# RMSNorm and matmul on one core: all loads from tile 16 on in halves of eight tiles, the last stores cut smaller

## The chip, the core and the metric

The kernel runs on one core of a Trainium2 chip. The metric is device time in microseconds (us), of which lower is better. A core has five engines with an instruction stream each: TensorE (PE) multiplies matrices, VectorE (DVE) and ScalarE (ACT) work element by element, GpSimd (POOL) casts here, and SyncE (SP) only issues transfers (DMAs) between the DRAM and the on-chip memory. All transfers of this kernel but one of 2 KB are issued from SP, in the order of its stream, and are carried out by 16 DMA engines.

## The reference

`x` has 16 x 1024 rows of 512 numbers, `weight` is 512 x 768, `gamma` has 512 numbers (ones), all in float32:

```
rms    = np.sqrt(np.mean(x ** 2, axis=-1, keepdims=True) + eps)
x_norm = x / rms * gamma
return np.matmul(x_norm, weight).astype(np.float32)
```

So 33.6 MB of `x` are read and 50.3 MB of output are written.

## The kernel before

The 16384 rows are worked on in NT = 128 tiles of 128 rows. A group of `x` has XG = 16 tiles (4 MB), a group of outputs OG = 8 tiles (3 MB). Inside a group of `x` a partition holds 16 consecutive rows, so that the part of one load or store that belongs to a partition is one stretch of DRAM: 32 KB for a load of 16 tiles, 16 KB for a load of 8, 24 KB for a store of 8 tiles, 12 KB for 4 and 6 KB for 2.

The path of a tile: the load brings `x` in float32 into one of two buffers `xt`. POOL casts it to bfloat16 (`cast`, L186, and `cast_quad`, L258). ACT squares it and sums each row (`square`, L194); for a batch of tiles ACT takes the root and DVE the reciprocal (`root`, L199 and L201). The cast rows are turned so that the features stand on the partitions: for twelve tiles of sixteen by PE (`transpose_word`, L228) with a copy by DVE (`evac`, L237), for the other four (a quad) by 16 block transposes on DVE (`move_quad`, L269). PE then multiplies with the weights (`matmuls`, L298), eight products for each tile, into one of three accumulators. Last, ACT (even tiles, L277) or DVE (odd tiles, L279) multiplies with the reciprocal root and writes to one of three buffers `ot` (`finish_tile`), and `store` (L291) issues the transfer out when the last tile of its stretch is done.

The order of all work is written out by hand in one list and given to the class `Order`. It finds from the cells that an operation reads and writes which earlier operations it has to wait for, leaves out waits that follow from waits already made, gives each transfer a semaphore slot, and emits the streams. `emit` returns the transfers that nobody waited for, and SP waits for those at the very end (L437).

Two tables say how the groups are cut. `x_size` gives the size of each load: group 0 goes in loads of 2, 2, 4 and 8 tiles, the groups 1, 2, 5, 6 and 7 in two loads of eight, and the groups 3 and 4 (tiles 48 to 63 and 64 to 79) in one load of sixteen. `o_size` gives the size of each store: group 0 in 2, 2, 4 tiles, group 1 in 4, 4, the last group (120 to 127) in 4, 4, all others in one store of eight.

Loop: `for j in range(1, NP)` works on a pair of tiles, 2j and 2j+1. `load_until` at its head issues the loads of a whole group as soon as the loop is 20 tiles or less ahead of it: the loads of group 3 stand in SP's stream behind the store of tiles 16 to 23, those of group 4 behind the store of tiles 32 to 39. A load waits until the tiles that lay in its buffer were read. The squares of pair j+4 are in ACT's stream ahead of the finish of tile 2j.

To keep a store to one wait, the finish of the last tile of a stretch also waits for the tile before it (`before` in `finish_tile`).

Of the kernel before, what the change touches and what calls it, by code (L numbers as in the profile page):

```python
# [20 lines left out]
class Order:  # L21
# [17 lines left out]
    def emit(self):  # L39
        nc = self.tc.nc  # L40
        streams = {id(e): n for n, e in enumerate((nc.tensor, nc.vector, nc.scalar, nc.gpsimd, nc.sync))}
        writer, readers = {}, {}
        known = [dict() for _ in streams]
        clocks, needs, place, slot_of, slots = [], [], [], {}, []
        count = [0] * len(streams)
        for n, (proc, engine, _, reads, writes) in enumerate(self.ops):
            at = streams[id(engine)]
            if proc is None:
                me, turn = ("transfer", n), 1
            else:  # L50
                count[at] += 1
                me, turn = at, count[at]
            written = {writer[cell] for cell in reads + writes if cell in writer}
            read = {d for cell in writes for d in readers.get(cell, ())}
            need = []
            for d in sorted(written | read, reverse=True):
                who, when = place[d]
                if who == me and (engine is nc.tensor or d not in written):
                    continue
                if known[at].get(who, 0) < when:  # L60
                    need.append(d)
                    for k, v in clocks[d].items():
                        known[at][k] = max(known[at].get(k, 0), v)
            if proc is None:
                free = [k for k, d in enumerate(slots) if known[at].get(("transfer", d), 0)]
                if free:
                    slots[free[0]] = n
                else:
                    slots.append(n)
                slot_of[n] = ("slot", slots.index(n))  # L70
            clock = dict(known[at])
            clock[me] = turn
            place.append((me, turn))
            clocks.append(clock)
            needs.append(need)
            for cell in reads:
                readers.setdefault(cell, []).append(n)
            for cell in writes:
                writer[cell], readers[cell] = n, []
        awaited = {d for need in needs for d in need}  # L80
        last = [n for n, (me, _) in enumerate(place) if not isinstance(me, int) and n not in awaited]
        sems, marks, done = {}, {}, {}
        for n in range(len(self.ops)):
            me = slot_of.get(n, place[n][0])
            if n in slot_of or n in awaited:
                if me not in sems:
                    sems[me] = self.tc.alloc_semaphore(f"done{len(sems)}")
                done[me] = done.get(me, 0) + (16 if n in slot_of else 1)
                marks[n] = (sems[me], done[me])
        for n, (proc, engine, issue, _, _) in enumerate(self.ops):  # L90
            for d in needs[n]:
                engine.wait_ge(*marks[d])  # L92
            ins = issue()
            if n in marks:
                ins.then_inc(marks[n][0], 16 if n in slot_of else 1)
        return [marks[n] for n in last]
# [3 lines left out]
def kernel(  # L100
# [18 lines left out]
    _, O = out.shape  # L119
    K = D // P  # L120
    NT = N // P
    NP = NT // 2
    XG, OG = 16, 8
    AHEAD = 20

    def stretches(group, parts):
        first, size, i = {}, {}, 0
        for g in range(NT // group):
            for n in parts.get(g, [group]):
                for t in range(i, i + n):  # L130
                    first[t], size[t] = i, n
                i += n
        return first, size

    last = NT // OG - 1
    x_first, x_size = stretches(XG, {0: [2, 2, 4, 8], **{g: [8, 8] for g in (1, 2, 5, 6, 7)}})
    o_first, o_size = stretches(OG, {0: [2, 2, 4], 1: [4, 4], last: [4, 4]})

    def rows(ap, i, n):
        base, t = (x_first[i], x_size[i]) if i < XG else (i - i % XG, XG)  # L140
# [332 lines left out]
```

## Time and profile before

| what | value |
|---|---|
| time, median of 5 runs (lowest to highest) | 209.91 us (209.66 to 210.12) |
| time of the profiled execution | 209.65 us |
| its span in the profile | 207.7 us |
| PE, DVE, ACT, POOL busy | 193.0, 149.3, 144.4, 59.9 us |
| DMA: bytes, mean rate | 85.62 MB, 412 GB/s |
| SP's queue (q1), share of 16 engines' span | 97.2% |
| transfers of x: 16 tiles / 8 tiles | 2 / 11 |
| stores: 8 / 4 / 2 tiles | 13 / 5 / 2 |
| last store issued | at 199.54 us |

The page cuts the span into 40 slices of 5.2 us. In the rows of digits 9 stands for 90% or more of a slice. "Idle before" names what an engine waited for last. The chain that ended last is followed back from the last instruction and says on which engine or transfer the time was spent. Beside that page the trace can be asked for the waits, for the busy time of each engine in any stretch, and for every instruction in order of time; it also holds a record of each DMA packet (start, duration, bytes) and of each landing: a transfer leaves 16 landings, one for each DMA engine.

### The profile page before, as it was taken

To read this page: it belongs to the slowest core of one execution; us is meant where nothing else is said; L and a number is where in the kernel's file an instruction comes from. 1 tells how busy PE (TensorE), PEld (TensorE's weight loads), DVE (VectorE), ACT (ScalarE), POOL (GpSimd) and SP (SyncE) were. 2 spreads that over 40 slices of the span, in tenths; PEclk is the share of its full clock that TensorE was granted. 3 is DMA by queue.
4 is the path that set the end of the run, shared out by engine and by line. 5 is a ranking of instruction groups with operands and counts; after the bars stand their busy time and mean duration, and the time that the engine had idled before them with its cause. 6 is when DMAs were issued, how large, how long until landed. Compare 5 with 4: busy or idle time off the path is not lost.

```text
span 207.7 us, 2760 instructions
## 1 busy us (share of the span) xinstructions
PE 193.0 (93%) x1212; PEld 72.3 (35%) x717; DVE 149.3 (72%) x255; ACT 144.4 (70%) x343; POOL 59.9 (29%) x34
## 2 busy tenths in 40 slices
PE   7789999999999999998999999999999999999920
PEld 1134444433334333342344333433343334343300
DVE  0455647998489956998569975999569984999410
ACT  4698897777768397865977688677877788663310
POOL 3247642046300192005800670006600273000000
PEclk9999999999999999999999999999999999999995
DMA  6999999999999999999999999999999999996995
GB/s 226 425 451 413 357 401 422 437 439 427 433 445 442 375 448 440 432 412 429 448 405 423 434 450 434 412 424 432 448 412 417 435 450 429 431 426 265 450 381 230
DMA packets 5488, 85.62 MB, mean 412 GB/s; under 512 B 610, under 2 KB 612, under 8 KB 1380
## 3 DMA queue, kind: packets, MB, share of 16 engines
q1 hardware_dynamic: 5472, 85.46, 97.2%
q8 instruction: 7, 0.11, 0.2%
q14 instruction: 5, 0.04, 0.0%
q10 hardware_dynamic: 4, 0.00, 0.0%
HBM read 35.13 MB, written 50.33 MB: 411 GB/s over the span
## 4 chain that ended last, share of the span: by engine, by line
PE 71%; DMA 16%; DVE 5%; issue 2%; SPq 1%; ACT 1%; POOL 1%; ACTq 0%
PE ps L298 62%; DMA xt<-in_x_dram 16%; PE ps L228 8%; DVE ot L279 2%; DVE xTq L269 2%; DVE xT L237 1%; POOL xb L186 1%; ACT jk L194 0%; SPq L343 0%; SPq L175 0%; ACT ot L277 0%; SPq L291 0%; DVE rstd L201 0%; SPq L468 0%; ACTq L92 0%
## 5 line engine op out<-in xcount | busy, mean ns | idle before, releaser
L298 PE MATMUL ps<-w_bf,xT 128*128 128x256 bf16 (+1 forms) x783 | 145.1, 325 | 2.7 <-DVE w_bf L279 0.8
L277 ACT ACTIVATE ot<-ps,rstd 128x768 f32<-128x768 f32 x64 | 57.5, 898 | 42.5 <-PE ps L298 40.8
L194 ACT ACTIVATE jk<-xt 128x512 bf16<-128x512 f32 x128 | 78.8, 619 | 7.8 <-DMA xt<-in_x_dram 7.8
L186 POOL CAST xb<-xt 128x2048 bf16<-128x2048 f32 (+3 forms) x21 | 46.3, 2221 | 112.3 <-DMA xt<-in_x_dram 94.8
L279 DVE TENSOR_SCALAR ot<-ps,rstd 128x768 f32<-128x768 f32 x64 | 64.8, 1013 | 9.6 <-PE ps L298 8.9
L294 PEld LDWEIGHTS <-xT 128*128 128x128 bf16 x400 | 39.3, 98 | 60.5 <-issue 52.4
L228 PE MATMUL ps<-ident_f,xb 128*128 128x128 f32 x200 | 54.2, 274 | 1.0 <-POOL xb L186 0.9
L237 DVE COPY xT<-ps 128x1024 bf16<-128x1024 bf16 (+1 forms) x53 | 34.5, 653 | 23.9 <-PE ps L228 22.2
L269 DVE STREAM_TRANSPOSE xTq<-xq 32x256 f32<-32x256 f32 x112 | 48.8, 435 | 3.4
L228 PEld LDWEIGHTS ps<-ident_f,xb 128*128 128x128 f32 x200 | 28.0, 141 | 46.6 <-issue 42.7
L298 PE MATMUL ps<-w_bf,xTq 128*128 128x256 bf16 (+1 forms) x217 | 41.8, 324 | 0.4
L194 ACT ACTIVATION_READ_ACCUMULATOR jk<-xt 128x1 f32 x128 | 24.3, 190 | 0.0
L294 PEld LDWEIGHTS <-xTq 128*128 128x128 bf16 x112 | 11.0, 98 | 14.5 <-issue 14.5
L258 POOL CAST xq<-xt 128x2048 bf16<-128x2048 f32 x7 | 13.3, 1897 | 0.0
L201 DVE RECIPROCAL rstd<-rms 128x8 f32<-128x8 f32 (+3 forms) x20 | 3.8, 192 | 8.4 <-ACT rms L199 8.2
L199 ACT ACTIVATE rms<-ssq,eps_sb 128x8 f32<-128x8 f32 (+3 forms) x20 | 6.0, 300 | 0.7
L298 PE MATMUL ps<-warm 128*128 128x512 bf16 x10 | 3.9, 531 | 1.4 <-DVE eps_sb L352 1.4
L277 ACT ACTIVATE w_bf<-w_f,g_sb 128x768 bf16<-128x768 f32 x2 | 1.9, 936 | 1.2 <-DMA w_f<-in_weight_dram 1.2
L375 DVE COPY g_sb<-ps 128x4 f32<-128x4 f32 x1 | 0.2, 161 | 3.1 <-PE ps L369 3.1
L339 ACT ACT_TABLE_LOAD x1 | 1.3, 1283 | 1.5 <-SPq L432 1.5
L279 DVE TENSOR_SCALAR w_bf<-w_f,g_sb 128x512 bf16<-128x512 f32 (+2 forms) x3 | 1.4, 481 | 0.7 <-DMA w_f<-in_weight_dram 0.7
L369 PEld LDWEIGHTS ps<-ident_f,g_row 2*128 2x128 f32 x2 | 0.3, 200 | 2.6 <-issue 2.6
(10 smaller groups left out, 1.9 us busy)
## 6 DMA issues: line engine op xcount, KB each, us to landing
out_dram<-ot SPq DMA_DIRECT2D x13, 3072.0 KB, 15.2
xt<-in_x_dram SPq DMA_DIRECT2D x11, 2048.0 KB, 19.7
xt<-in_x_dram SPq DMA_DIRECT2D x2, 4096.0 KB, 23.5
out_dram<-ot SPq DMA_DIRECT2D x5, 1536.0 KB, 11.2
w_f<-in_weight_dram SPq DMA_DIRECT2D x2, 768.0 KB, 5.6
out_dram<-ot SPq DMA_DIRECT2D x2, 768.0 KB, 15.9
xt<-in_x_dram SPq DMA_DIRECT2D x2, 512.0 KB, 5.2
xt<-in_x_dram SPq DMA_DIRECT2D x1, 1024.0 KB, 9.1
```

The costliest lines, as they stand in the source:

```text
L186: run(POOL, lambda: POOL.tensor_copy(out=xb[s][:, i % 8:i % 8 + n, :], in_=src), of, cells("xb", s, i % 8, n))
L194: run(ACT, lambda: ACT.activation(out=jk[j], in_=src[:, 0, :], func=AF.Square, accum_out=ssq[:, i:i + 1]), of, [("jk", j), ("ssq", i)])
L199: run(ACT, lambda: ACT.activation(out=rms[:, s], in_=ssq[:, s], func=AF.Sqrt, scale=1.0 / D, bias=eps_sb), [("ssq", t) for t in range(i, i ...
L201: run(DVE, lambda: DVE.reciprocal(out=rstd[:, s], in_=rms[:, s]), [("rms", i)], [("rstd", t) for t in range(i, i + n)])
L228: run(PE, lambda: PE.transpose(out=tp[b][:, t, h, :], in_=words[:, lo:lo + P], identity=ident_f), cells("xb", s, j % 4 * 2 + t) + ["ident" ...
L237: run(DVE, lambda: DVE.tensor_copy(out=dst[:, t:t + n, :], in_=src[:, t:t + n, :]), [("tp", b)], cells("xT", j % 4, t, n))
L258: run(POOL, lambda: POOL.tensor_copy(out=xq[s], in_=src), of, [("xq", s)])
L269: run(DVE, lambda: DVE.transpose(out=dst, in_=src), [("xq", s)], [("xTq", s)])
L277: run(ACT, lambda: ACT.mul(out=dst, in_=src, mul=r), reads, writes)
L279: run(DVE, lambda: DVE.tensor_single_scalar(out=dst, in_=src, scalar=r, op=mybir.AluOpType.mult), reads, writes)
L294: run(PE, lambda: PE.ldweights(lhsT), [cell])
L298: run(PE, lambda: PE.add_instruction(mybir.InstMatmult(name=nc.get_next_instruction_name(), engine=mybir.EngineType.PE, ins=[PE.lower_ap(r ...
```

## The change

Three places. The groups 3 and 4 of `x` are loaded in two loads of eight tiles, as the others are. The store of tiles 112 to 119 is cut into two of four tiles, and the second of the last group (124 to 127) into two of two tiles. And `emit` decides in another way which transfers are left for SP to wait for at the end: those whose completion stands in no engine's `known` clock, in place of those that no operation waits for.

```
-        last = [n for n, (me, _) in enumerate(place) if not isinstance(me, int) and n not in awaited]
+        seen = {who for clock in known for who in clock}
+        last = [n for n, (me, _) in enumerate(place) if me not in seen and not isinstance(me, int)]
...
-    x_first, x_size = stretches(XG, {0: [2, 2, 4, 8], **{g: [8, 8] for g in (1, 2, 5, 6, 7)}})
-    o_first, o_size = stretches(OG, {0: [2, 2, 4], 1: [4, 4], last: [4, 4]})
+    x_first, x_size = stretches(XG, {0: [2, 2, 4, 8], **{g: [8, 8] for g in range(1, NT // XG)}})
+    o_first, o_size = stretches(OG, {0: [2, 2, 4], 1: [4, 4], last - 1: [4, 4], last: [4, 2, 2]})
```

## The prediction

> **What bounds the kernel now.** I began with the page: busy shares, the slices, the queues.
>
> ```profile
> PE 193.0 (93%) x1212; PEld 72.3 (35%) x717; DVE 149.3 (72%) x255; ACT 144.4 (70%) x343; POOL 59.9 (29%) x34
> ...
> DMA  6999999999999999999999999999999999996995
> GB/s 226 425 451 413 357 401 422 437 439 427 433 445 442 375 448 440 432 412 429 448 405 423 434 450 434 412 424 432 448 412 417 435 450 429 431 426 265 450 381 230
> ...
> q1 hardware_dynamic: 5472, 85.46, 97.2%
> ...
> PE 71%; DMA 16%; DVE 5%; issue 2%; SPq 1%; ACT 1%; POOL 1%; ACTq 0%
> ```
>
> PE is busy for 93%, and the chain names it for 71%. But SP's queue fills the 16 DMA engines for 97.2%; from the second to the 36th slice the DMA row has only nines. Two resources are nearly full, and the question is which sets the end. PE's last product ends at about 198.5 us, DVE finishes tile 127 at 199.51, and the last landing is at 206.30. So I looked at the only hole of the DMA row, the 37th slice, us by us (columns: stretch, length, busy time and count of each engine, clock, DMA share, GB/s):
>
> ```profile
> 186.00:187.00 1.00, 0.97 (x7) 0.34 (x4) 0.97 (x2) 0.43 (x1) 0.00 (x0) 1.00 0.91 393
> 187.00:188.00 1.00, 0.98 (x7) 0.40 (x4) 0.92 (x3) 0.47 (x1) 0.00 (x0) 1.00 0.69 295
> 188.00:189.00 1.00, 1.00 (x8) 0.29 (x3) 0.95 (x2) 0.00 (x0) 0.00 (x0) 1.00 0.46 197
> 189.00:190.00 1.00, 1.00 (x8) 0.29 (x3) 0.97 (x2) 0.61 (x1) 0.00 (x0) 1.00 0.17 74
> 190.00:191.00 1.00, 1.00 (x8) 0.29 (x3) 0.93 (x3) 0.29 (x1) 0.00 (x0) 1.00 0.98 418
> ```
>
> The share falls step by step, 0.91, 0.69, 0.46, 0.17: the engines run dry one after another, not together. The landings say the same. Of the store of tiles 104 to 111 the first engine's part lands at 187.51, the median at 189.09, the last at 191.47. The packet records say why. In 13 stores of eight tiles nearly every 24 KB packet took 912 ns, but on one engine, in an unbroken chain, 92 packets had a mean of 945 ns; its 12 KB packets took 482 where the others' took 460. This late engine loses 8 x 0.033 = 0.26 us in each such store, 3.4 us over 13, so its 3.96 us of delay are explained. It closes its part of that store at 190.98 us; two others, delayed by instruction fetches and slow packets, at 190.81 and 190.72. The next store (tiles 112 to 119) was issued at 189.78 and its first packets start at 190.6. Thirteen engines had stood idle; the late one went on without a pause, and it is last in every later landing: 198.97, 202.68, 206.30, each 0.6 us behind the field. The end of the kernel is this one engine's queue, full from 2 us to the end.
>
> **The change part by part.**
>
> *Groups 3 and 4 in halves.* Here the waits around 60 to 100 us:
>
> ```profile
> POOL xb L186 <- DMA xt<-in_x_dram: 35.0, 2, 18.0
> ...
> ACT jk L194 <- DMA xt<-in_x_dram: 5.4, 2, 3.0
> ...
> PE ps L298 <- ACT ot L277: 0.7, 1, 0.7
> ```
>
> ACT's first square of group 3 waits 2.38 us for its load, that of group 4 3.00 us (ready at 92.94, load landed at 95.86); behind it stands the finish of tile 56, and PE misses its accumulator for 0.7 us. A load of 16 tiles is eight packets of 1213 ns on each engine, 9.7 us; its first half lands 4.9 us sooner, so both ACT waits go, and PE's 0.7 us. What is late next? The transfers: each store would be issued up to 0.7 us sooner, but a store waits 7 us or more behind others (median 15.2 us to landing where eight packets of 912 ns are 7.3). PE's 0.7 us is worth nothing at the end as long as the queue is full. The last store is issued at 199.54 and the late engine reaches its packets at about 205.8 - 8 x 0.48 = 202.0: some 2 us of cover. Were that gone, the 0.7 us would count in full.
>
> The price: two packets of 16 KB for one of 32, 2 x 611 - 1213 = 9 ns, eight times, and one closing packet of 9 ns for each further transfer: 0.08 us on each engine for a group, 0.16 for both. SP issues a second load in about 0.87 us (0.86 and 0.87 where a group is halved today); the store next in its stream waits for a tile some 10 us later (59.07 after 48.55), so nobody is kept. POOL and ACT wait once more for each group, on a load that in the halved groups lands before the square comes round: 0, covered until the second half comes over 4 tiles, 6 us, late.
>
> *Tiles 112 to 119 in two stores.* The store of 112 to 115 is issued when DVE is done with tile 115, at 183.45 us, 6.3 us sooner, and fills the hole: 0.09 + 0.31 + 0.54 + 0.83 = 1.8 us of mean idle. But it fills it on the engines that were early. On the late engine the same bytes follow without a pause now, so its gain is 0, and its price is the packets': 16 x 482 against 8 x 945 ns and one closing packet, 0.16 us. A gain of 190.98 - 190.62 = 0.36 us, down to the others' start, would be there only for the 0.6 us by which it ends last, and needs it to be less late: excluded from the sum, kept in a rival.
>
> *Tiles 124 to 127 in two stores.* Tiles 124 and 125 leave when DVE is done with 125, at 196.9, not 199.5; the late engine then still has the stores ahead until 202. So again no gain. 6 KB packets: 234 ns against 460 for 12 KB, 8 ns a pair elsewhere; for the late engine no row shows 6 KB packets in a full write queue, so from 2 x 241 (the slowest ordinary one at 28 us) to 2 x 256 (its 22 ns added to each): 0.0 to 0.24 us. I take 0.07, nearest to the 8 ns a pair.
>
> The two cut stores add a wait of DVE on ACT at tile 115 and at 125: ACT is done with 114 at 181.40 before DVE starts at 182.43, and with 124 at 195.49 before 195.89. Cost 0, with 0.4 us of margin in the second. On SP nothing but the next stores is queued behind the new ones.
>
> *Fewer waits at the end.* A transfer enters a `known` clock only when an operation waits for it or inherits that from one that did. So "in nobody's clock" and "waited for by nobody" are the same set, and this edit does nothing. The unawaited stores are those of the last use of each `ot` buffer: four before, six after. The extra waits are met while the last store is under way: SP waits 5.9 us for that one. Cost 0; the 207.7 - 206.3 = 1.4 us after the last landing stay.
>
> *Sum on the late engine:* 0.16 + 0.16 + 0.07 = 0.39, say +0.4 us (0.3 to 0.6). From the profiled 209.65 that is 210.05; its time is 0.26 under the median of 209.91, and it is the median that will be compared, so 210.3.
>
> The Trainium skill speaks louder against the change: "SBUF: State Buffer", section "The DMA setup-cost knee", gives every transfer a fixed cost of about 2 us and says to coalesce into the largest transfer; four more would make 8 us by it, an estimate of 217.9. The rows here stand against that: in the full queue a closing packet takes 9 ns and the next transfer's first packet starts at once.
>
> **The rivals.**
>
> *Faster: the hole counts.* If the late engine's delay were less in the runs than in the profile, or the engines shared their delay, filling the hole would bring the mean idle of 1.8 us, less 0.4: 208.5. At most the last 768 KB store would be bound by PE: issue 198.8, 0.5 to its first packet, eight of 234 ns, 0.5 to land, 202.1, or 4 us less. For it: the hole is real, and the mean of the 16 engines is 1.8 us early. Against it: the last landing follows the late engine without a pause, and the runs without a profile (209.66 and up) are not faster than the profiled one, as they would be if it were less late there.
>
> *Slower: a read stall on a late engine.* Single load packets took up to twice their time at moments when the other engines turned from a load to a store, and hit engines already late: +0.54 us at 47 us, +1.06 and +0.83 at 68, +0.61 at 142. Every transfer after 48 us is now timed anew. If one more such stall falls on any of the three late engines (two stand only 0.3 and 0.4 us behind the last), it goes straight to the end: 0.4 + 0.5 to 1.1, that is 210.8 to 211.4. It decides from a stall of 0.3 us on. It can also go the other way, as the one at 68 us fell into a 4 MB load that is now cut.
>
> *It does not do what it says.* For the waits I hold that as certain, and it is in the sum.
>
> **How the numbers follow.** What a measurement here can tell from no change is about 0.2%, 0.42 us. Forecast (late engine bound, +0.3 to +0.6 with a spread of the runs of 0.25): 0.60, its own range 209.9 to 210.9; of that 0.36 lies within 0.42 us and 0.24 above. Hole counts: 0.24, 206.1 to 209.0, mostly near 208.5. Stall: 0.14. The rest, 0.02, no change. So faster 0.24, same 0.38, slower 0.38. The range from 208.3 to 211.1 leaves out some 0.10 of the second case and 0.05 of the third.
>
> **What would show it.** Right: PE's wait of 0.7 us and ACT's of 3.0 and 2.38 us gone; the DMA share at 0.9 or more from 186 to 191 us; the engines then running dry at the very end, the share falling over the last 4 us before the last landing and that store's 16 landings spread by about 4 us instead of 0.6, with the last one still near 206.5. Wrong: a last landing below 205.7 with its 16 landings close together (the hole counted), or a late engine more than 4.5 us behind (the stall).

## The result, and the profile after

Median 210.18 us (209.93 to 211.7, 22 runs) against 209.88 us for the kernel before (209.51 to 210.5, 40 runs): a ratio of 1.002, 95% interval 1.0011 to 1.003. The kernel became slower by 0.3 us going by the medians, by 0.2 to 0.6 us going by the ratio: clear of zero, and about as much as the 0.2% that the prediction counted as no change. Two of the 22 runs took 211.47 and 211.7 us, where none of the 40 runs of the kernel before took more than 210.5. Beside later kernels it was timed once more: 1.0014 (1.0001 to 1.0027). The profiled execution took 210.05 us with a span of 208.0.

The page after: busy shares, the DMA rows of the slices, SP's queue, and the chain by engine.

```profile
PE 193.5 (93%) x1212; PEld 72.8 (35%) x717; DVE 149.3 (72%) x255; ACT 144.7 (70%) x343; POOL 60.0 (29%) x34
...
DMA  6999999999999999999999999999999999999991
GB/s 224 381 444 422 394 411 424 446 429 424 440 418 432 435 424 430 433 427 425 429 422 427 451 419 438 421 419 441 424 432 435 430 414 443 440 421 416 423 396 65
...
q1 hardware_dynamic: 6048, 85.46, 97.2%
...
PE 88%; DMA 5%; SPq 1%; issue 1%; POOL 1%; DVE 0%
```

The hole of the 37th slice is gone, and nothing was won by it. Note the chain: it gives PE 88% now, although PE does not set the end (experiment e5). The chain follows an instruction's waits; that a transfer lay in a full queue is not in it.

Us by us, the stretch where the hole was and the end (columns as before):

```profile
186.00:187.00 1.00, 0.95 (x7) 0.41 (x4) 0.93 (x3) 0.88 (x1) 0.00 (x0) 1.00 0.97 418
187.00:188.00 1.00, 1.00 (x9) 0.32 (x5) 0.94 (x3) 0.02 (x1) 0.00 (x0) 1.00 1.01 430
188.00:189.00 1.00, 1.00 (x8) 0.32 (x4) 0.97 (x2) 0.06 (x1) 0.00 (x0) 1.00 0.98 418
189.00:190.00 1.00, 1.00 (x8) 0.32 (x4) 0.93 (x3) 0.84 (x1) 0.00 (x0) 1.00 1.07 455
...
202.00:203.00 1.00, 0.00 (x0) 0.00 (x0) 0.00 (x0) 0.00 (x0) 0.00 (x0) 0.50 0.72 301
203.00:204.00 1.00, 0.00 (x0) 0.00 (x0) 0.00 (x0) 0.00 (x0) 0.00 (x0) 0.50 0.41 172
204.00:205.00 1.00, 0.00 (x0) 0.00 (x0) 0.00 (x0) 0.00 (x0) 0.00 (x0) 0.50 0.15 61
205.00:206.00 1.00, 0.00 (x0) 0.00 (x0) 0.00 (x0) 0.00 (x0) 0.00 (x0) 0.50 0.10 43
```

The staircase that stood at 186 to 190 us (0.91, 0.69, 0.46, 0.17) has moved to the very end: 0.72, 0.41, 0.15, 0.10. The engines run dry one after another there. The 16 landings of the last store run from 202.58 to 206.43, over 3.85 us; before, from 205.70 to 206.30. Fourteen engines finish sooner by 0.8 us or more, the last two, at 206.12 and 206.43, do not. The slow chain of store packets is there as before: 92 packets of 24 KB with a mean of 945 ns.

### The profile page after: what moved, and what is told of

The parts are those of the page before. It is cut to its first block, busy times and chain, and to the rows that moved or that the text cites. A ratio compares the mean times of both kernels' runs of the same rounds, so it can differ in the third digit from the quotient of the medians.

```text
span 208.0 us, 2771 instructions
## 1 busy us (share of the span) xinstructions
PE 193.5 (93%) x1212; PEld 72.8 (35%) x717; DVE 149.3 (72%) x255; ACT 144.7 (70%) x343; POOL 60.0 (29%) x34
## 4 chain that ended last, share of the span: by engine, by line
PE 88%; DMA 5%; SPq 1%; issue 1%; POOL 1%; DVE 0%
PE ps L299 78%; PE ps L229 10%; DMA xt<-in_x_dram 5%; POOL xb L187 1%; DVE ot L280 0%; SPq L344 0%; SPq L176 0%; SPq L469 0%; SPq L433 0%
## 5 line engine op out<-in xcount | busy, mean ns | idle before, releaser
L299 PE MATMUL ps<-warm 128*128 128x512 bf16 x10 | 4.8, 627 | 1.4 <-DVE eps_sb L353 1.4
```

The source lines that it names most:

```text
L299: run(PE, lambda: PE.add_instruction(mybir.InstMatmult(name=nc.get_next_instruction_name(), engine=mybir.EngineType.PE, ins=[PE.lower_ap(r ...
```

## The experiments

Each kernel is named by its difference. A ratio is to the kernel before, timed on the same chip.

**e1: the loads alone**

```
-    ... {g: [8, 8] for g in (1, 2, 5, 6, 7)}
+    ... {g: [8, 8] for g in range(1, NT // XG)}
```

> The kernel before with one part of the change: groups 3 and 4 of x in two loads of eight. Theory (the end is set by the latest of the 16 DMA engines, whose queue is full from 2 us on): PE's 0.7 us wait near 97 us is gone, and nothing of it reaches the end; two further transfers cost 2 x 0.08 us, so +0.0 to +0.3 us against before, and the hole in the DMA share near 188 us stays or grows by up to 0.7 us. Rival (PE's chain sets the end): 0.7 us less.

Measured: 1.0008 (0.9996 to 1.0019), 209.95 us. PE's wait of 0.7 us on ACT is gone from its waits, and so are ACT's two waits for the whole loads. ACT's waits for loads over the whole span were, in the kernel before,

```profile
ACT jk L194 <- DMA xt<-in_x_dram: 7.8, 5, 3.0
```

and here they are

```profile
ACT jk L194 <- DMA xt<-in_x_dram: 3.0, 3, 1.7
```

Tile 127 is done at 198.46 instead of 199.51, 1.05 us sooner; the last landing is at 206.28 instead of 206.30. The hole is still there (a DMA share of 0.63 and 0.52 from 187 to 189 us). A sooner PE is worth nothing at the end. The interval rules out the rival's 0.7 us.

**e2: the stores alone**

```
-    ... 1: [4, 4], last: [4, 4]})
+    ... 1: [4, 4], last - 1: [4, 4], last: [4, 2, 2]})
```

> The kernel before with the other part alone: tiles 112 to 119 stored in 4, 4 and 120 to 127 in 4, 2, 2. Theory of the latest engine: the hole near 188 us is filled, the landings of the last store are spread by about 4 us instead of 0.6, and the last landing stays: +0.0 to +0.4 us. Rival (the hole counts): 1.4 to 1.8 us less.

Measured: 1.0012 (0.9998 to 1.0027), 210.01 us. Its end, us by us:

```profile
202.00:203.00 1.00, 0.00 (x0) 0.00 (x0) 0.00 (x0) 0.00 (x0) 0.00 (x0) 0.50 0.98 406
203.00:204.00 1.00, 0.00 (x0) 0.00 (x0) 0.00 (x0) 0.00 (x0) 0.00 (x0) 0.50 0.46 190
204.00:205.00 1.00, 0.00 (x0) 0.00 (x0) 0.00 (x0) 0.00 (x0) 0.00 (x0) 0.50 0.19 80
205.00:206.00 1.00, 0.00 (x0) 0.00 (x0) 0.00 (x0) 0.00 (x0) 0.00 (x0) 0.50 0.12 49
```

The hole is filled (0.90 or more from 185 to 191 us), the staircase stands at the end, and the last store's landings go from 203.28 to 206.79. The 1.4 to 1.8 us of the rival are ruled out.

The third part, the rule for the last waits, had no run of its own. By the code of `emit`, the old and the new rule pick the same transfers, four in the kernel before and six in the kernel after, and nothing else depends on the rule.

**e4: less in the queue**

```
-        if i == first + n - 1:
+        if i == first + n - 1 and i != 63:
```

> The kernel after without the store of tiles 56 to 63, whose rows stay unwritten: 3 MB less in the queue near 95 us, 7.3 us of work for an ordinary engine and 7.6 us for the late one. Theory of the latest engine: the queue's end moves forward until PE binds: last store issued at about 199, then 0.5 us to its first packet, eight of 0.24 us and 0.5 us to land, so 3.5 to 4 us less than after. Rival (PE's chain sets the end): under 0.5 us less.

Measured: 205.76 us, 0.98 (0.9783 to 0.9817), so 4.4 us under the kernel after, a little more than the 3.5 to 4 that were expected. Its last us:

```profile
200.00:201.00 1.00, 0.00 (x0) 0.00 (x0) 0.00 (x0) 0.00 (x0) 0.00 (x0) 0.53 1.05 436
201.00:202.00 1.00, 0.00 (x0) 0.00 (x0) 0.00 (x0) 0.00 (x0) 0.00 (x0) 0.50 0.54 215
202.00:203.00 1.00, 0.00 (x0) 0.00 (x0) 0.00 (x0) 0.00 (x0) 0.00 (x0) 0.50 0.00 0
```

The share stays at 1.05 and drops to nothing within one us: all 16 landings of the last store lie between 201.94 and 202.16. The queue ran dry before (a share of 0.01 from 193 to 194 us), and the engines started level. Now PE sets the end: the store of tiles 120 to 123 is issued when tile 123 is done, at 193.27, and from there the last packets follow one another to the end. The work of PE is the same and 3 MB less are in the queue. That 4.4 us are to be had this way shows that the queue bounds the kernel after; PE comes next, 4.4 us below it.

**e5: more on PE**

```
+            if i == 100:
+                hold(warm[:, :P], "warm")
+                for _ in range(10):
+                    product(ops[a][:, :WIDE], warm[:, :P], warm, True, True, ["warm"], [("ops", a, 0)])
             matmuls(i, a, range(K), feed)
```

> The kernel after with one more weight load and ten more products of 512 columns on PE ahead of tile 100, written into an accumulator that is overwritten next: 2.2 us of PE work more at about 155 us. Theory of the latest engine: PE and the last store's issue are 2.2 us later, the last store still reaches the late engine before that has worked off its queue (4 us of cover), and the time is as in after, within 0.3 us. Rival (PE's chain sets the end): 2.2 us more.

Measured: 210.23 us, 1.001 (0.9998 to 1.0022); the kernel after has 210.18. PE is busy for 196.1 us instead of 193.5. The end in order of time:

```profile
199.52 1.02 DVE L280 TENSOR_SCALAR ot<-ps,rstd 128x768 f32<-128x768 f32 x1 [1.58 <-PE ps L299]
200.56 0.33 SPq L292 DMA_DIRECT2D out_dram<-ot  x1
```

Of the 2.6 us, 1.5 reach the end of PE's work: the last store is issued at 200.56 instead of 199.09, not 2.2 us later as was expected. The last landing comes 6 us after that issue, at 206.80, and the time of the runs is that of the kernel after. An engine that is 93% busy took 2.6 us more work, and finished 1.5 us later, for nothing; the interval excludes 1.5 us more. With e4 this settles what binds: each of the two resources was changed by itself, and only the queue moved the time.

**e7: the price of a transfer**

```
+            for p in range(first, first + n, 2 if n == OG else n):
+                m = 2 if n == OG else n
+                src = ot[s][:, p % OG:p % OG + m, :]
+                order.transfer(SP, ... rows(out, p, m) ..., reads=cells("ot", s, p % OG, m))
```

> The kernel after with each of the 12 stores of eight tiles (tiles 16 to 111) issued as four transfers of two tiles one behind the other, at the place in SP's stream where the one stood: 36 transfers more, and no load is pushed back. It prices a transfer in the full queue. By the packets (8 x (4 x 234 - 912) and three closing packets of 9 ns): 0.22 us for each store on an ordinary engine, 2.6 us over all; on the late engine between 0 and 6 us. So 2 to 4 us above after, PE without a new stall. By a fixed cost of about 2 us each: 72 us.

Measured: 214.4 us, 1.021 (1.017 to 1.0251). The kernel before had 210.1 on that chip, so the kernel after would have had about 210.4: 4.0 us for 36 transfers, 0.11 us each. On the first engine the last landing moved from 202.58 to 204.89, 2.3 us (2.6 were worked out); on the last one from 206.43 to 210.35, 3.9 us. PE waited more than was expected (2.4 us for ACT), but the DMA share is 0.97 or more from 184 to 193 us, so the queue covered it. So a transfer in a full queue costs its packets, not 2 us.

**e3: the same cuts in another place**

```
-    ... 1: [4, 4], last: [4, 4]})
+    ... 1: [4, 4], **{g: [2, 2, 2, 2] for g in range(2, last + 1)}})
```

> The kernel before with all stores from tile 16 on in pieces of two tiles: 41 transfers more, in size as the last two of the change. Theory (a transfer costs a full queue only its packets): on the late engine 0.18 to 0.66 us for each of 13 cut stores, on the others 0.22, so 2.5 to 8 us more, most likely 3 to 5. By a fixed cost of about 2 us for each transfer: 80 us more. If filling the queue sooner were worth something: less than before.

Measured: 1.0292 (1.0264 to 1.0319), 216.34 us. That is 6.4 us, inside the expected 2.5 to 8, but packets alone are not the reason, for PE stalls here. SP's queue, and the wait behind it:

```profile
35.67 20.71 SPq L291 DMA_DIRECT2D out_dram<-ot  x8
56.42 1.10 SPq L175 DMA_DIRECT2D xt<-in_x_dram  x1
```

```profile
PE ps L298 <- ACT ot L277: 6.7, 3, 5.6
```

SP issues in order. A store of two tiles is waited for at each pair, so group 3's load, which stood behind the store of tile 23, now stands behind that of tile 29 and is issued at 56.42 instead of 48.55. The move of the loads is in this number together with the 41 transfers; e7, where the four transfers are issued at the old place, gives the price of the transfers alone. The change itself is free of this: no load follows the stores that it cuts.

**e6: taking the late engine out**

```
+            low = 0
+            for high in CUTS.get(first, []) + [P]:
+                order.transfer(SP, ... rows(out, first, n)[low:high], in_=src[low:high] ...)
+                low = high
...
+    CUTS = {32: [120], 48: [126], 64: [104], 80: [108], 96: [110]}
```

> The kernel after with five stores of eight tiles each cut by partitions into two transfers, so that ever fewer DMA engines may take part: tiles 32 to 39 as 120 and 8 partitions, 48 to 55 as 126 and 2, 64 to 71 as 104 and 24, 80 to 87 as 108 and 20, 96 to 103 as 110 and 18. If the number of engines is the largest up to 16 that divides the partitions, and the first ones are taken, the engines left out get 8 to 10 packets of 24 KB less in each, and the first two 12 more over all, 10.9 us. Theory of the latest engine: the time is now set by the first engines, 7 us (if the late engines are among the last) to 11 us (if they are among the first) above after. Rival (the mean of the engines or PE sets the end): under 2 us more.

Measured: 256.29 us, 1.221 (1.2181 to 1.2238), 46 us more than before, far outside both expectations. Its DMA rows:

```profile
DMA  6999999999999989999999898998986669994840
GB/s 261 439 435 389 373 435 431 414 444 422 433 431 288 292 318 396 420 348 351 351 405 375 295 342 317 387 351 277 318 308 282 243 188 255 321 359 191 355 193 17
```

From the first such store on (72 us) the engines are busy but slow: 9 at 288 GB/s. In the packet records, 263 of the 1291 packets of 24 KB after 75 us took more than one and a half times 912 ns, with a mean of 2.06 us. The number of engines was as assumed: the transfer of 120 partitions leaves 15 landings beside one update at its issue, that of 8 leaves eight beside one. (The Trainium skill, "DMA: Bandwidth & Descriptors", section "Why a DMA increments its semaphore by 16 and not by 1", gives that rule: the number of engines is the largest up to 16 that divides the partitions, and the issuing engine writes the rest of the 16 at once. These counts agree with it, and so do those of the other four stores.) Why the packets collide was not tried, and which of the 16 is the late engine stays open.

**e8: the same cut where every engine runs dry**

```
 (as e4)
-    ... last - 1: [4, 4], last: [4, 2, 2]})
+    ... last: [4, 4]})
```

> The kernel after without the store of tiles 56 to 63 (rows unwritten, as before in e4_store_left_out) and with the uncut last stores of the kernel before (120 to 127 in 4 and 4, 112 to 119 in one). Where no engine is late, the cut of the last store should be worth what it promises: this kernel ends with 1.5 MB after PE is done where e4_store_left_out ends with 0.75 MB, so 1.6 to 2.0 us slower than that. If the cut is worth nothing whether or not an engine is late: equal to it.

Measured: 208.27 us, 0.9908 (0.988 to 0.9936), against 0.98 for e4: 2.3 us slower by the ratios, 2.7 by the last landings (204.89 and 202.16), more than the 1.6 to 2.0 that were expected. The expectation counted the last store alone, but the hole counts as well: here 16.1 us lie between the issue of the uncut store of tiles 112 to 119, at 188.81, and the last landing, while in e4 8.9 us lie between the issue of the store of tiles 120 to 123, at 193.27, and the last landing. The share in the hole:

```profile
185.00:186.00 1.00, 1.00 (x8) 0.37 (x5) 0.97 (x2) 0.40 (x1) 0.00 (x0) 1.00 0.12 49
186.00:187.00 1.00, 0.95 (x7) 0.40 (x4) 0.93 (x3) 0.50 (x1) 0.00 (x0) 1.00 0.00 0
187.00:188.00 1.00, 1.00 (x8) 0.29 (x3) 0.94 (x3) 0.00 (x0) 0.00 (x0) 1.00 0.00 0
188.00:189.00 1.00, 1.00 (x8) 0.29 (x3) 0.97 (x2) 0.58 (x1) 0.00 (x0) 1.00 0.00 0
```

Here no engine has work for three us. One is still late, for the landings of tiles 104 to 111 run from 184.84 to 186.61, but its part too has landed 2.2 us before the next store is issued. In the kernel before the share fell no lower than 0.17: three engines in sixteen were still busy, and that made the same cut worthless.

**e9 and e10: fewer transfers, and where the cover ends.** If transfers cost and PE is covered, fewer of them should be faster than both kernels.

```
 (e9, from the kernel before)
-    ... {g: [8, 8] for g in (1, 2, 5, 6, 7)}
-    ... {0: [2, 2, 4], 1: [4, 4], last: [4, 4]}
+    ... {g: [8, 8] for g in (1, 2, 7)}
+    ... {0: [2, 2, 4], last: [4, 4]}
 (e10: the same with)
+    ... {0: [2, 2, 4], last - 1: [4, 4], last: [4, 2, 2]}
```

> The kernel before turned the other way: groups 3, 4, 5 and 6 of x each in one load of sixteen tiles, and tiles 8 to 15 stored in one piece, so three transfers fewer than before. Theory (a full queue pays for packets, PE has some 2 us of cover): at 0.08 to 0.11 us each, 0.2 to 0.4 us less than before, although ACT waits 2 to 3 us for each whole load and PE up to 0.7 us. Rival (the waits of PE count): 0.7 to 1.5 us more.

> e9_fewer_transfers with the cut last stores of the kernel after (112 to 119 in 4, 4; 124 to 127 in 2, 2). In e9 PE is 3.3 us later, and the store of tiles 112 to 119, issued at 193.0, came after even the late engine had run dry. Theory: with that store cut, its first half is there in time, the queue stays full, and the time is that of the late engine again, as in after, 210.0 to 210.5. If instead PE's 3.3 us count whatever the cut: 212 and more.

Measured: e9 212.18 us, 1.0097 (1.0079 to 1.0115); e10 210.46 us, 1.0019 (1.0003 to 1.0034). The expectation for e9 was wrong: tile 127 is done 3.3 us later than before, and this time it counts. PE waits 3.4 us for ACT instead of 0.7, and at the start 0.6 us more for the weights. Around the hole of e9:

```profile
189.00:190.00 1.00, 1.00 (x9) 0.45 (x5) 0.97 (x2) 0.17 (x1) 0.00 (x0) 1.00 0.29 123
190.00:191.00 1.00, 1.00 (x9) 0.36 (x4) 0.93 (x3) 0.74 (x1) 0.00 (x0) 1.00 0.12 49
191.00:192.00 1.00, 1.00 (x7) 0.29 (x3) 0.94 (x2) 0.00 (x0) 0.00 (x0) 1.00 0.00 0
192.00:193.00 1.00, 1.00 (x8) 0.30 (x4) 1.00 (x1) 0.35 (x1) 0.00 (x0) 1.00 0.00 0
```

The uncut store of tiles 112 to 119 is issued only at 193.05, when even the late engine is dry; from there 14.7 us of packets follow. In the kernel before, the late engine went on to this store at 190.98, 0.4 us after the first packets of it had started, so 2.9 of the 3.3 us should reach the end. The last landing is at 209.14, 2.84 us later than before. With that store cut, in e10, the first half is there in time:

```profile
189.00:190.00 1.00, 0.99 (x7) 0.40 (x4) 0.90 (x3) 0.46 (x1) 0.00 (x0) 1.00 0.87 369
190.00:191.00 1.00, 1.00 (x8) 0.29 (x3) 0.97 (x2) 0.00 (x0) 0.00 (x0) 1.00 1.04 442
```

The queue as a whole does not stay full in e10: the share is 0.70 and 0.73 from 191 to 193 us and 0.35 from 196 to 197. The last engine's queue does: from the store of tiles 104 to 111 on, the last landings of the stores are at 191.94, 195.71, 199.46, 203.21, 205.07 and 206.89, one stretch of packets after another. The other fifteen engines land the last store between 205.01 and 205.49.

So the cut of the tail is worth nothing in the kernel before, 2.3 us in e8, and e10 is 1.6 us faster than e9. Not all of that is the cut's: in the profile of e10 tile 127 is done 2.0 us later than before, not 3.3. PE's wait for ACT is 2.7 us there instead of 3.4, which is 0.7 of the difference; the rest was not followed. None of the kernels that do the whole computation beat the kernel before.

**e11: the kernel after again**

> The kernel after once more, beside e10 on the same chip: 210.1 to 210.4, 1.0011 to 1.003 of the kernel before.

Measured: 210.25 us, 1.0014 (1.0001 to 1.0027). Its last store's landings run from 202.38 to 206.63.

## Why the prediction was right, step by step

- *What binds.* Right, and shown: the queue (e4, -4.4 us), not PE (e5, no change). The late engine is no matter of one execution: in the profiles of before, after, e1, e2, e5, e9, e10 and e11 the last engine's part of the store of tiles 104 to 111 lands 3.0 to 4.5 us behind the first one's. Why one engine is slower is open.
- *The halves of groups 3 and 4.* Right: the waits are gone, PE is sooner, the end is not (e1).
- *The cut of tiles 112 to 119 and of 124 to 127.* Right: the hole is filled on the engines that were early, and the last engine's queue is unchanged (e2; landings of the kernel after). The condition that the prediction gave, that a late engine still has work when the next store comes, is shown by its opposite in e8.
- *The rival "hole counts".* Ruled out for this kernel by e2. It holds as soon as all engines run dry (e8, e9). The 202.1 us in the prediction's bound for it is added up wrongly: its terms make 201.7, so the low end of that rival's range, 206.1, stands 0.4 us too high. No result of the change comes near it.
- *The rival "stall".* The last engine's part of the store of tiles 104 to 111 landed at 191.54 instead of 191.47: no further stall fell on it in the profiled execution. The two runs of 211.47 and 211.7 us are as slow as the rival said or slower, but no profile was taken of them, so whether a stall fell there is not shown.
- *The waits at the end.* The rule does nothing, as was said.
- *The sum.* 0.39 us was put on the late engine's packets: 0.16 for the two loads, 0.23 for the cut stores. The 0.23 is the term that was mis-sized, for the cut stores cost next to nothing. From the last landing of the store of tiles 104 to 111 to the end it is 14.83 us in the kernel before and 14.78 in e1, with the stores uncut; it is 14.89 in the kernel after, 14.69 in its second profile (e11) and 14.87 in e2. The prediction took 482 ns for a packet of 12 KB on the late engine. Its own landings, 198.97, 202.68 and 206.30, leave 3.71 and 3.62 us for eight such packets, some 460 ns each. In the kernel after, the late engine works off the two stores of tiles 112 to 119 in 3.75 us each, which together is the 7.50 us of the one store before.
- *The loads' 0.16 us.* The profiles can't tell it. The store of tiles 104 to 111 lands last at 191.47 in the kernel before and at 191.50 in e1, at 191.54 and 191.94 in the two profiles of the kernel after, and at 191.92 in e2, which has the old loads.
- *"The 1.4 us after the last landing stay."* They did not: from the last landing to SP's closing drain it takes 0.91 us in the four profiles with four unawaited stores (before, e1, e8, e9) and 1.05 us in those with six (after, e2, e4, e5, e10, e11). So 0.23 us were put where there is almost nothing, and nothing was put where there are 0.14. The two errors cancel in part. That the forecast of 210.3 is 0.1 us from the median of 210.18 is partly luck, the more so as the last landing of the kernel after is 0.13 us later than before in one profile and 0.33 in the other.
- *"Some 2 us of cover".* Taken at the wrong place. It was worked out at the last store. The tightest place of the kernel before is the store of tiles 112 to 119: issued at 189.78, first packets at 190.6, the late engine done at 190.98, which leaves some 0.4 us. It did not matter for the forecast, since PE only became sooner; it made the expectation for e9 wrong.

## What to carry to other kernels

Where a transfer queue is full from the first us on, ask the landings, not the mean share, who is last: a hole in the mean of 16 engines is worth only what it is on the latest one. Filling such a hole, or speeding an engine that works ahead of it, buys no time but slack, and how much slack is read at the store where the queue comes nearest to dry. To find what binds when two resources stand above 90%, take a little from each by itself and see which moves the end.

## What was not expected of the hardware

- The 16 DMA engines drift apart over a run. In the kernel before, one took 945 ns for the 24 KB packets that took 912 on the others. Seven instruction fetches of 16 KB took 0.92 to 1.5 us each on the engine that they fell on, and the packet beside most of them 0.4 us more. At 191 us the first and the last engine are 4 us apart.
- Cutting five stores unevenly by partitions made a fifth of the 24 KB packets after 75 us take 2.06 us on the mean in place of 912 ns (e6) and cost 46 us; why is open.
- The time from the last landing to the end grew by 0.14 us with the cut tail. In the kernels compared, the two further waits and the smaller last store came together, and they were not separated. In e7 and e3, which have nine and twelve unawaited stores and the smaller last store, it is 1.08 and 1.07 us, so it does not grow by the number of waits.
